# Seven block products in 18 of 44 weight units of a down projection (hybrid decoder block, one core)

## The chip, the cores and the metric

The kernel runs on 1 core of one Trainium2 chip. The metric is the device time of one execution in microseconds (us). Three executions of the kernel before took 1677.74, 1678.96 and 1675.05 us, median 1677.74 us. The profile comes from one further execution, which took 1675.62 us.

## The reference

One decoder layer, 256 tokens, model width 2048, feed-forward width 5632, all in float32: two token mixers, then a gated MLP with a short causal convolution, then a gate on a per-layer embedding. The change touches the MLP's last product, its residual sum, and the code that makes its left operand `h`:

```
h   = gelu(causal_conv3(x @ w_gate)) * (x @ w_up)     # 256 x 5632
ffn = h @ w_down                                      # 5632 x 2048
x   = layer_norm(ALPHA * x + ffn)
x   = x + sigmoid(x @ w_ple_gate) * (p @ w_ple_proj)
```

## The kernel before

All weights come from DRAM in 284 **units** of 128 x 2048 floats (1 MB) in one array `wu`, in the order in which they are used. TensorE (PE) works on a float32 value as a sum of a rounded part `hi` and a remainder `lo`, and forms three of the four products of two such sums. `prep` (L120) prepares a unit in two halves of 128 x 1024: SyncE (SP) loads `raw` (L126), ScalarE (ACT) copies it to `hi` (the copy is L104), VectorE (DVE) writes `lo = raw - hi` (L130). `unit` (L138) prepares up to unit u+2 before unit u is used. Four `raw` buffers hold two units, six `hi` and six `lo` buffers hold three. Nothing else is in front of PE: it waits only for `hi` and `lo`.

**The MLP** makes 44 blocks of 128 channels of `h`, number n = 0 to 43. For each, 16 K tiles of `w_gate` and of `w_up` go through PE into `psg` and `psu`, GpSimd (POOL) copies edge columns (`gp`, L998), DVE and ACT do convolution, gelu and product, and a tile `hT` gets the block's hi and lo parts for 256 tokens (L1013 is the last DVE operation).

**The down projection** is `residual("dn", ...)` (L831) with `x_half` (L251). It runs units 224 to 267, in two halves `nh` = 0 and 1 of the output's columns, 22 units each, i = 0 to 21. Unit i of a half holds the K tiles 2i and 2i+1 (256 channels of `h`) against 1024 output columns. `x_mm` (L223, the matmul is L237) does 24 matmuls for a unit: 2 K tiles, 2 halves of 128 tokens, 2 halves of 512 columns, and the three products ah*hi, ah*lo, al*hi; each has a 128 x 128 block of `h` as weights and 512 columns of the unit moving. Four PSUM banks collect the four blocks 128 tokens x 512 columns of a half. At its end `ev` (L834) does z = ALPHA*z + bank (L838) and the layer norm's statistics (L839) on DVE for each bank. `z` is the residual stream; its two tiles of 1 MB come back from the DRAM copy `x1d` with the layer norm's gains `lnb` (2 MB more) in `mid2` (L1020), which SP issues after unit i = 4 of the first half. The operands of the embedding's projection (`praw`, `pTr`; `ple_prep`, L859) are loaded at i = 17 of the second half. The last two units of that half are worked bank by bank (the tail), so that the layer norm's chain (L751 to L762), the transposes `ptl` (L765) and the embedding's products (`pp`) lie between the last matmuls. Then the gate's units follow (`pg`).

Each engine works its instructions in program order; a DMA that SP or POOL issues waits in that engine's order too. The order on SP is that of the program, the others' is a scheduler's.

Of the kernel before, what the change touches and what calls it, by code (L numbers as in the profile page):

```python
# [9 lines left out]
F32 = mybir.dt.float32  # L10
F32R = mybir.dt.float32r
# [3 lines left out]
ALU = mybir.AluOpType  # L15
# [4 lines left out]
P = 128  # L20
# [3 lines left out]
NF = DFF // P  # L24
# [4 lines left out]
ALPHA = 2 ** 0.25  # L29
# [12 lines left out]
LPAD = 24  # L42
XSTAT = (*range(32, 64), *range(120, 136), *range(224, 284))
S8W = 2048
WH = 1152
HSTEP = 48

# [5 lines left out]
def tile_block(ctx: ExitStack, tc: tile.TileContext, wu, wfv, wpp, xT_in, x_in, pT_in, wlr,  # L53
               chan, gnorm, lng, ident_in, mask_in, cmask_in, out):
    nc = tc.nc
# [4 lines left out]
    ring = ctx.enter_context(tc.tile_pool(name="ring", bufs=4))  # L60
# [33 lines left out]
    def t2(name):  # L94
        return sm.tile([P, 512], F32, tag="t2", bufs=6, name=name)

    def mmtile(name):
        return pmm.tile([P, 512], F32, tag="mm", name=name)

    def mxtile(name):  # L100
        return pmx.tile([P, 512], F32, tag="mx", name=name)

    def copy(o, i, scale=1.0):
        nc.scalar.activation(o, i, AF.Copy, bias=0.0, scale=scale)  # L104
# [12 lines left out]
    n_prep = [0]  # L117
    ready = {}

    def prep():  # L120
        u = n_prep[0]
        n_prep[0] += 1
        his, los = [], []
        for h in range(2):
            raw = ring.tile([P, 1024], F32, tag="raw", bufs=4, name=f"raw{u}_{h}")
            nc.sync.dma_start(raw, wu[u, :, h * 1024:(h + 1) * 1024])  # L126
            hi = w_tile("hi", F32R, f"hi{u}_{h}", u)
            copy(hi, raw)
            lo = w_tile("lo", F32R, f"lo{u}_{h}", u)
            nc.vector.tensor_tensor(lo, raw, hi.bitcast(F32), ALU.subtract)  # L130
            his.append(hi)
            los.append(lo)
        ready[u] = (his, los)
# [90 lines left out]
    def x_mm(banks, w, a, toks, first, last, cs=(0, 1), part=None):  # L224
# [3 lines left out]
        for t in toks:  # L228
            ah = a[:, t * P:t * P + P]
            al = a[:, 256 + t * P:256 + t * P + P]  # L230
            for i, (x, v) in enumerate(((ah, hi), (ah, lo), (al, hi))):
                for c in cs:
                    bs = banks[t][c]
                    m = 512 // len(bs)
                    for j in range(len(bs)) if part is None else (part,):
                        o = c * 512 + j * m
                        nc.tensor.matmul(bs[j][:, 0:m], lhsT=x, rhs=v[:, o:o + m],  # L237
                                         start=first and i == 0, stop=last and i == 2)

    mixers = []  # L240

    def pull(n):
# [6 lines left out]
                    mixers.pop(0)  # L249

    def x_half(name, act, K, evac, pulls=0, head=0, tail=0, mid=None, done=None, end=None,  # L251
               fine=False):
# [12 lines left out]

        us = [unit() for _ in range(head)]
        for t in range(2):
            for i, w in enumerate(us):
                mm(i, w, (t,))
        for i in range(head, n - tail):  # L270
            mm(i, unit(), (0, 1))
            pull(pulls)
            if mid is not None and i == mid[1]:
                mid[0]()
        us = [unit() for _ in range(tail)]

        def tail_mm(t, c, i):
            mm(n - tail + i, us[i], (t,), (c,))
            if i == tail - 1:
                evac(t, c, banks[t][c][0])  # L280

        if end is not None:
            end(tail_mm)
            return
        for t in range(2):
            for c in range(2):
                bs = banks[t][c]
                for j, ps in enumerate(bs):
                    for i, w in enumerate(us):
                        mm(n - tail + i, w, (t,), (c,), j)  # L290
                    if len(bs) == 1:
                        evac(t, c, ps)
                    else:
                        evac(t, c, ps[:, 0:256], (256 * j, 256 * j + 256))
            if done is not None:
                done(t)
# [531 lines left out]

        return stat, norm, turn

    def residual(name, act, K, zs, stats, mid, done=None, end=None):  # L831

        for nh in range(2):
            def ev(t, c, ps, nh=nh):  # L834
                g = 2 * nh + c
                zc = zs[t][:, g * 512:g * 512 + 512]
                with tc.high_priority(P_STAT):
                    nc.vector.scalar_tensor_tensor(zc, zc, ALPHA, ps, ALU.mult, ALU.add)  # L838
                    nc.vector.bn_stats(stats[t][:, g, :], zc)  # L839
            x_half(f"{name}{nh}", act, K, ev, tail=2 if nh == 1 else 0, mid=(mid[nh], 4 if nh == 0 else K // 2 - 5),  # L840
                   done=done if nh == 1 else None, end=end if nh == 1 else None)

    def affine(zs, gb_, after, gs=range(4)):
        for t in range(2):
# [130 lines left out]
    for i in range(2):  # L975
        nc.gpsimd.memset(gp[i][:, 0:2], 0.0)
    hT = [None] * 11

    def lt(shape, dt, name):
        return late.tile(shape, dt, name=name)  # L980
# [9 lines left out]
    for n in range(NF):  # L990
        if n % 4 == 0:
            hT[n // 4] = (s8 if n < 40 else lt)([P, 4, 512], F32R, name=f"hT{n // 4}")
        psg = gate_up(f"psg{n}")
        g = gp[n % 2]
        comb(psg, g[:, 2:258])
        cw = [chn[:, c_cw + j * NF + n:c_cw + j * NF + n + 1] for j in range(3)]
        for i in range(2):
            nc.gpsimd.tensor_copy(g[:, 258 + i:259 + i], g[:, 129 - i:130 - i])  # L998
# [12 lines left out]
        dst = hT[n // 4][:, n % 4, :]  # L1011
        copy(dst[:, 0:256], y)
        nc.vector.tensor_tensor(dst[:, 256:512], y, dst[:, 0:256].bitcast(F32), ALU.subtract)  # L1013
        if n >= 4:
            pull(1)

# [3 lines left out]
    def mid2():  # L1020
        for t in range(2):
            nc.sync.dma_start(z2[t], x1d[t])
        gain[1] = load_gain(1)

    x2T = [s8([P, 4, 512], F32R, name=f"x2T{g}") for g in range(4)]
# [4 lines left out]
            pb.extend(ple_proj(1, *pq[0]))  # L1030
        ln_out(z2, st2, t, x2T, c_g2, c_b2, "l2", P_LN2[t])

    residual("dn", hT, NF, z2, st2, (mid2, lambda: pq.append(ple_prep(1))), done2)
    pp = [s8([P, 2, 1024], name=f"ppk{i}") for i in range(2)]
    for t in range(2):
        for c in range(2):
# [112 lines left out]
```

## Time and profile before

| | |
|---|---|
| time of the profiled execution | 1675.62 us |
| span of the profile | 1673.6 us |
| median of three other executions | 1677.74 us |
| granted TensorE clock | 1.0 in all slices |
| PE, DVE, ACT, POOL busy | 99%, 66%, 50%, 2% |
| dn matmuls, first to last start | 1056, from 1331.4 to 1572.7 us |

About 2.0 us of the profiled time lie outside its span. "Busy" counts an engine's instructions; PE's matmuls overlap one another, so what a matmul costs is read from the distance of starts, not from its length. In the views an operation stands as line, engine, operation, output<-input with buffer numbers left out, and the shapes; "idle before <-" is the time in which an engine waited and what it waited for.

### The profile page before, as it was taken

The page shows a single profiled execution, that of the slowest core. Times are in us where ns is not written, and L with a number is a line of the kernel's source. Part 1 is how long each engine was busy: PE and PEld are TensorE (multiplying, and loading weights), DVE is VectorE, ACT ScalarE, POOL GpSimd, SP SyncE. Part 2 cuts the span into 40 slices and gives each one's busy share as a digit, 9 for nine tenths or more (in the row PEclk, how much of TensorE's full clock was granted, in tenths as well). Part 3 has the DMA queues.
Part 4 walks back from the last instruction along what each step waited for, and adds up shares of the span by engine and source line. Part 5 has one row for each costly group of instructions (what it writes and reads, how often), then busy time and mean ns, then how long its engine had stood idle before and what let it go on. Part 6 is the DMA issues. An engine that isn't in the chain of part 4 may idle for free.

```text
span 1673.6 us, 23839 instructions
## 1 busy us (share of the span) xinstructions
PE 1663.7 (99%) x9035; PEld 1442.6 (86%) x9035; DVE 1097.6 (66%) x1588; ACT 833.7 (50%) x1200; POOL 36.0 (2%) x123
## 2 busy tenths in 40 slices
PE   9999999999999999999999999999999999999998
PEld 8888888888888888888888888888888888888887
DVE  6576658768756657774687776677676644545774
ACT  5655545545555554443465545555545434334633
POOL 0100000000000000000010000000000000000000
PEclk9999999999999999999999999999999999999999
DMA  7765555555555556567746665555555575566454
GB/s 268 258 201 165 165 188 184 180 177 177 184 180 175 167 191 196 193 195 279 237 159 201 219 221 193 193 195 191 194 196 193 194 295 191 193 194 206 154 182 170
DMA packets 91426, 330.22 MB, mean 197 GB/s; under 512 B 10232, under 2 KB 11904, under 8 KB 89904
## 3 DMA queue, kind: packets, MB, share of 16 engines
q1 hardware_dynamic: 90528, 324.51, 58.3%
q0 software_dynamic: 784, 4.20, 0.7%
q8 instruction: 70, 1.15, 0.3%
q14 instruction: 44, 0.36, 0.1%
HBM read 323.42 MB, written 5.25 MB: 196 GB/s over the span
## 4 chain that ended last, share of the span: by engine, by line
PE 97%; DVE 1%; ACT 0%; DMA 0%; SPq 0%; issue 0%; POOL 0%; ACTq 0%
PE dn L237 14%; PE psu L193 9%; PE psg L193 9%; PE psm L193 7%; PE gr L237 5%; PE gv L237 5%; PE wo L237 5%; PE pg L237 5%; PE psu L195 5%; PE psg L195 5%; PE psm L195 3%; PE psa L193 3%; PE fv L344 2%; PE psfk L193 2%; PE psq L193 2%; PE psfq L193 2%
## 5 line engine op out<-in xcount | busy, mean ns | idle before, releaser
L130 DVE TENSOR_TENSOR lo<-raw,hi 128x1024 fp32r<-128x1024 f32 x568 | 694.0, 1224 | 484.6 <-ACT hi L104 483.5
L104 ACT ACTIVATE hi<-raw 128x1024 fp32r<-128x1024 f32 x568 | 601.8, 1060 | 706.9 <-issue 260.0
L193 PE MATMUL psu<-x1T,hi 128*128 128x512 f32 x688 | 236.0, 389 | 0.0
L193 PE MATMUL psg<-x1T,hi 128*128 128x512 f32 x672 | 230.5, 389 | 0.0
L237 PE MATMUL dn<-hi,hT 128*128 128x512 f32 x704 | 190.0, 389 | 0.0
L195 PE MATMUL psu<-x1T,lo 128*128 128x256 f32 x688 | 189.9, 276 | 0.0
L195 PE MATMUL psg<-x1T,lo 128*128 128x256 f32 x672 | 185.5, 276 | 0.0
L193 PE MATMUL psm<-xT,hi 128*128 128x512 f32 x512 | 175.8, 391 | 0.0
L237 PEld LDWEIGHTS dn<-hi,hT 128*128 128x128 f32 x704 | 132.1, 188 | 27.4
L193 PEld LDWEIGHTS psu<-x1T,hi 128*128 128x128 f32 x688 | 129.1, 188 | 26.8
L193 PEld LDWEIGHTS psg<-x1T,hi 128*128 128x128 f32 x672 | 126.2, 188 | 26.2
L195 PE MATMUL psm<-xT,lo 128*128 128x256 f32 x512 | 141.4, 276 | 0.0
L195 PEld LDWEIGHTS psu<-x1T,lo 128*128 128x128 f32 x688 | 129.1, 188 | 0.0
L195 PEld LDWEIGHTS psg<-x1T,lo 128*128 128x128 f32 x672 | 126.1, 188 | 0.0
L193 PEld LDWEIGHTS psm<-xT,hi 128*128 128x128 f32 x512 | 96.1, 188 | 19.8
L237 PE MATMUL dn<-lo,hT 128*128 128x512 f32 x352 | 109.7, 389 | 0.0
L195 PEld LDWEIGHTS psm<-xT,lo 128*128 128x128 f32 x512 | 96.1, 188 | 0.1
L193 PE MATMUL psa<-oT,hi 128*128 128x512 f32 x256 | 87.8, 389 | 0.0
L237 PEld LDWEIGHTS dn<-lo,hT 128*128 128x128 f32 x352 | 66.1, 188 | 13.7
L237 PE MATMUL gv<-hi,xT 128*128 128x512 f32 x256 | 72.3, 394 | 0.0
L237 PE MATMUL gr<-hi,xT 128*128 128x512 f32 x256 | 72.1, 394 | 0.0
L195 PE MATMUL psa<-oT,lo 128*128 128x256 f32 x256 | 70.7, 276 | 0.0
(247 smaller groups left out, 2423.3 us busy)
## 6 DMA issues: line engine op xcount, KB each, us to landing
raw<-in_wu_dram SPq DMA_DIRECT2D x568, 512.0 KB, 4.6
fvraw<-in_wfv_dram SPq DMA_DIRECT2D x14, 524.0 KB, 8.9
lnb<-in_lng_dram SPq DMA_DIRECT2D x4, 1024.0 KB, 12.0
z<-in_x_dram SPq DMA_DIRECT2D x2, 1024.0 KB, 7.6
praw<-in_wpp_dram SPq DMA_DIRECT2D x4, 512.0 KB, 3.8
x1d<-z POOLq DMA_DIRECT2D x2, 1024.0 KB, 7.5
z<-x1d SPq DMA_DIRECT2D x2, 1024.0 KB, 7.6
xraw<-in_xT_dram SPq DMA_DIRECT2D x7, 256.0 KB, 7.7
```

What stands on the lines that cost most here:

```text
L104: nc.scalar.activation(o, i, AF.Copy, bias=0.0, scale=scale)
L130: nc.vector.tensor_tensor(lo, raw, hi.bitcast(F32), ALU.subtract)
L193: nc.tensor.matmul(ps, lhsT=hi[i // 8 if hoff == 0 else 0][:, w0 % 1024:w0 % 1024 + P], rhs=a[:, kt % 4, :], start=first and i == 0, stop= ...
L195: nc.tensor.matmul(ps[:, 256:512], lhsT=lo[i // 8 if hoff == 0 else 0][:, w0 % 1024:w0 % 1024 + P], rhs=a[:, kt % 4, 0:256], start=False, ...
L237: nc.tensor.matmul(bs[j][:, 0:m], lhsT=x, rhs=v[:, o:o + m], start=first and i == 0, stop=last and i == 2)
L344: nc.tensor.matmul(fbk[t][c][:, 0:n], lhsT=x, rhs=w[:, o:o + n], start=kt == 0 and i == 0, stop=kt == 15 and i == 2)
```

## The change

In nine units of each half (i = 2, 4, ... 18; `DNP`) the 256 x 1024 block of `w_down` and the 256 x 256 block of `h` are taken as 2 x 2 matrices of blocks, and the product is formed from **seven** block products instead of eight (the Winograd form of Strassen's scheme). Each takes three matmuls of 128 x 128 by 128 x 512, so such a unit has 21 in place of 24. Three of the seven add into the half's own banks; four (`ms`) collect in banks of their own over the nine units, so that all eight banks of PSUM are in use from i = 2 to 18.

- `prep_seven` makes the operands. ACT copies 512 + 1024 columns to `hi` and, for the weights' four combinations, 2 x 1024 to a tile `ts`; DVE makes `lo` of 512 + 1024, four combinations of 512 in place in `raw`, and 2 x 1024 `lo` parts of `ts`. `ts` takes the wide S8 buffers.
- h's four combinations are made once, in the MLP, at n = 5, 9, ... 37: four DVE operations of 128 x 128, an ACT copy and a DVE subtraction of 128 x 512, and two POOL writes of 256 KB to DRAM (`hsd`). Each seven unit loads them back with two POOL DMAs of 256 KB, into the free upper halves of its first `hi` and `lo`.
- `joined` adds the four banks onto z after i = 18: one ACT copy and eight DVE operations of 128 x 512. z is scaled by ALPHA there, so `ev` only adds.
- `mid2` loads z alone; the gains' 2 MB move to i = 17 of the second half, behind `ple_prep`.

```
+DN0 = 224
+DNP = tuple(range(2, 20, 2))
...
+    def prep_seven(u):
...
+            n = 512 * (h + 1)
+            copy(hi[:, 0:n], raw[:, 0:n])
+            nc.vector.tensor_tensor(lo[:, 0:n], raw[:, 0:n], hi[:, 0:n].bitcast(F32),
+                                    ALU.subtract)
...
+        sums[u](his[0][:, 512:1024], los[0][:, 512:1024])
+        (b11, b12), (b21, b22) = [(r[:, 0:512], r[:, 512:1024]) for r in raws]
+        nc.vector.tensor_tensor(b11, b12, b11, ALU.subtract)
+        nc.vector.tensor_tensor(b12, b22, b12, ALU.subtract)
+        nc.vector.tensor_tensor(b22, b22, b11, ALU.subtract)
+        nc.vector.tensor_tensor(b21, b21, b22, ALU.subtract)
+        ts = []
+        for h, raw in enumerate(raws):
+            t = s8([P, 2, 1024], F32R, name=f"ts{u}_{h}")
+            copy(t[:, 0, :], raw)
+            nc.vector.tensor_tensor(t[:, 1, :], raw, t[:, 0, :].bitcast(F32), ALU.subtract)
+            ts.append(t)
...
+    def seven(banks, ms, w, act, kt, first, last):
...
+        for ps, (xh, xl), (vh, vl) in (
+                (ms[0], x[0], (h0[:, 0:512], l0[:, 0:512])),
+                (banks[0][0][0], x[1], (h1[:, 0:512], l1[:, 0:512])),
+                (banks[0][1][0], s[3], (h1[:, 512:1024], l1[:, 512:1024])),
+                (ms[1], s[0], t1_), (ms[2], s[2], t3), (ms[3], s[1], t2_),
+                (banks[1][0][0], x[2], t4)):
+            m = any(ps is p for p in ms)
+            for i, (a, v) in enumerate(((xh, vh), (xh, vl), (xl, vh))):
+                nc.tensor.matmul(ps, lhsT=a, rhs=v, start=m and first and i == 0,
+                                 stop=m and last and i == 2)
...
+            if i in ws:
...
+                seven(banks, ms, unit(), act, 2 * i, i == ws[0], i == ws[-1])
+                if i == ws[-1]:
+                    joined(ms)
+            else:
+                mm(i, unit(), (0, 1))
...
-                    nc.vector.scalar_tensor_tensor(zc, zc, ALPHA, ps, ALU.mult, ALU.add)
+                    if ws:
+                        nc.vector.tensor_tensor(zc, zc, ps, ALU.add)
...
+            def joined(ms, zp=zp):
+                p1, p5, p7, p6 = ms
+                u = t2("ju")
+                copy(u, p1)
...
+                onto(0, 0, p1)
+                plus(u, u, p6)
+                onto(0, 1, u)
+                plus(u, u, p7)
+                onto(1, 0, u)
+                plus(u, u, p5)
+                onto(1, 1, u)
+                plus(zp(0, 1), zp(0, 1), p5)
...
+            nc.gpsimd.dma_start(h.bitcast(F32), hsd[j, :, 0, :])
+            nc.gpsimd.dma_start(l.bitcast(F32), hsd[j, :, 1, :])
...
+        if n % 2 == 1 and n // 2 in DNP:
+            sf = t2("hs")
+            x_sums(before[0], y, sf)
...
+                nc.gpsimd.dma_start(hsd[DNP.index(n // 2), :, i, :], sp.bitcast(F32))
...
+    def mid2b():
+        pq.append(ple_prep(1))
         gain[1] = load_gain(1)
...
+    residual("dn", hT, NF, z2, st2, (mid2, mid2b), done2, ws=DNP)
```

Where the changed order matters:

**DVE, first half, one seven unit with the regular unit behind it.** Before, a unit is two rows of `lo`, four for two units:

```order
L130 TENSOR_TENSOR lo_0_14039<-raw_0_14035,hi_0_14037 128x1024
L130 TENSOR_TENSOR lo_1_14045<-raw_1_14041,hi_1_14043 128x1024
L130 TENSOR_TENSOR lo_0_14075<-raw_0_14071,hi_0_14073 128x1024
L130 TENSOR_TENSOR lo_1_14081<-raw_1_14077,hi_1_14079 128x1024
```

Now (L133, L140 to L143 and L148 are the seven unit's, the two L165 the next, regular unit's):

```order
L133 TENSOR_TENSOR lo_0_13436<-raw_0_13433,hi_0_13435 128x512
L140 TENSOR_TENSOR raw_0_13433<-raw_0_13433 128x512
L141 TENSOR_TENSOR raw_0_13433<-raw_1_13439,raw_0_13433 128x512
L133 TENSOR_TENSOR lo_1_13442<-raw_1_13439,hi_1_13441 128x1024
L148 TENSOR_TENSOR ts_0_13451<-raw_0_13433,ts_0_13451 128x1024
L142 TENSOR_TENSOR raw_1_13439<-raw_1_13439,raw_0_13433 128x512
L165 TENSOR_TENSOR lo_0_13482<-raw_0_13478,hi_0_13480 128x1024
L143 TENSOR_TENSOR raw_1_13439<-raw_1_13439 128x512
L165 TENSOR_TENSOR lo_1_13488<-raw_1_13484,hi_1_13486 128x1024
L148 TENSOR_TENSOR ts_1_13454<-raw_1_13439,ts_1_13454 128x1024
```

Ten rows stand where four stood. The seven unit's first `raw` buffer is free for the next seven unit's load only after L142, its last operand `ts_1` is made behind both halves of the regular unit.

**SP, around the loads of z.** Before:

```order
L126 DMA raw_1_12907<-in_wu_dram 128x1024
L1022 DMA z_12746<-x1d 128x2048
L1022 DMA z_12747<-x1d 128x2048
L856 DMA lnb_12939<-in_lng_dram 128x2048
L856 DMA lnb_12940<-in_lng_dram 128x2048
L126 DMA raw_0_12943<-in_wu_dram 128x1024
```

Now (L128 loads a seven unit's half, L161 a regular one's; the numbers are the units'):

```order
L128 DMA raw230_0_13026<-in_wu_dram 128x1024
L128 DMA raw230_1_13032<-in_wu_dram 128x1024
L1151 DMA z20_12846<-x1d_7192 128x2048
L1151 DMA z21_12847<-x1d_7192 128x2048
L161 DMA raw231_0_13073<-in_wu_dram 128x1024
L161 DMA raw231_1_13079<-in_wu_dram 128x1024
L128 DMA raw232_0_13109<-in_wu_dram 128x1024
```

The two `lnb` loads are gone from this place. Before, the two issues of z waited for the MLP's last matmul. Now the first waits for PE's last product with `ts` of unit 226 and the second for PE's product with the first `ts` of unit 228 (z takes buffers that `ts` tiles held), and `raw231` and what follows stand behind them on SP.

**DVE, at the end of the second half's seven units** (i = 18 is unit 264; `ju` is the sum that `joined` carries). Now:

```order
L926 SCALAR_TENSOR_TENSOR z_12846<-z_12846,dn1m_13842 128x512
L930 TENSOR_TENSOR ju<-ju,dn1m_13845 128x512
L926 SCALAR_TENSOR_TENSOR z_12846<-z_12846,ju 128x512
L930 TENSOR_TENSOR ju<-ju,dn1m_13844 128x512
L926 SCALAR_TENSOR_TENSOR z_12847<-z_12847,ju 128x512
L930 TENSOR_TENSOR ju<-ju,dn1m_13843 128x512
L930 TENSOR_TENSOR z_12846<-z_12846,dn1m_13843 128x512
L926 SCALAR_TENSOR_TENSOR z_12847<-z_12847,ju 128x512
```

These eight rows did not exist; they stand ahead of `lo` of units 266 and 267, the two units of the tail.

More of the change, by code (lines that the diff above doesn't have):

```diff
@@ L118, in tile_block @@
     ready = {}
+    sums = {}
+    def prep_seven(u):
+        raws, his, los = [], [], []
+        for h in range(2):
+            raw = ring.tile([P, 1024], F32, tag="raw", bufs=4, name=f"raw{u}_{h}")
+            nc.sync.dma_start(raw, wu[u, :, h * 1024:(h + 1) * 1024])
+            hi = w_tile("hi", F32R, f"hi{u}_{h}", u)
+            lo = w_tile("lo", F32R, f"lo{u}_{h}", u)
+            n = 512 * (h + 1)
+            copy(hi[:, 0:n], raw[:, 0:n])
+            nc.vector.tensor_tensor(lo[:, 0:n], raw[:, 0:n], hi[:, 0:n].bitcast(F32),
+                                    ALU.subtract)
+            raws.append(raw)
+            his.append(hi)
+            los.append(lo)
+        sums[u](his[0][:, 512:1024], los[0][:, 512:1024])
[10 more added lines that the diff above has]
+            ts.append(t)
+        ready[u] = (his, los, ts)
     def prep():
@@ L122, in prep @@
         n_prep[0] += 1
+        if u in sums:
+            prep_seven(u)
+            return
         his, los = [], []
@@ L238, in x_mm, with x_sums @@
                                          start=first and i == 0, stop=last and i == 2)
+    def seven(banks, ms, w, act, kt, first, last):
+        (h0, h1), (l0, l1), ts = w
+        a0, a1 = [act[k // 4][:, k % 4, :] for k in (kt, kt + 1)]
+        x = [(a[:, t * P:t * P + P], a[:, 256 + t * P:256 + t * P + P])
+             for a, t in ((a0, 0), (a1, 0), (a1, 1))]
+        s = [(h0[:, 512 + i * P:512 + i * P + P], l0[:, 512 + i * P:512 + i * P + P])
+             for i in range(4)]
+        t1_, t3, t4, t2_ = [(t[:, 0, o:o + 512], t[:, 1, o:o + 512])
+                            for t in ts for o in (0, 512)]
+        for ps, (xh, xl), (vh, vl) in (
[8 more added lines that the diff above has]
+                                 stop=m and last and i == 2)
+    def x_sums(ae, ao, o):
+        d = [o[:, i * P:i * P + P] for i in range(4)]
+        a11, a21, a12, a22 = ae[:, 0:P], ae[:, P:256], ao[:, 0:P], ao[:, P:256]
+        for dst, a, b, op in ((d[0], a21, a22, ALU.add), (d[1], d[0], a11, ALU.subtract),
+                              (d[2], a11, a21, ALU.subtract), (d[3], a12, d[1], ALU.subtract)):
+            nc.vector.tensor_tensor(dst, a, b, op)
     mixers = []
@@ L270, in x_half @@
         for i in range(head, n - tail):
-            mm(i, unit(), (0, 1))
+            if i in ws:
+                if i == ws[0]:
+                    ms.extend(mmtile(f"{name}m{j}") if j % 2 == 0 else mxtile(f"{name}m{j}")
+                              for j in range(4))
+                seven(banks, ms, unit(), act, 2 * i, i == ws[0], i == ws[-1])
[3 more added lines that the diff above has]
+                mm(i, unit(), (0, 1))
             pull(pulls)
@@ L977, in tile_block, with h_sums, load @@
     hT = [None] * 11
+    hsd = dr.tile([len(DNP), P, 2, 512], F32, name="hsd")
+    before = [None]
+    def h_sums(i):
+        j = DNP.index(i)
+        def load(h, l):
+            nc.gpsimd.dma_start(h.bitcast(F32), hsd[j, :, 0, :])
+            nc.gpsimd.dma_start(l.bitcast(F32), hsd[j, :, 1, :])
+        return load
+    for nh in range(2):
+        for i in DNP:
+            sums[DN0 + nh * (NF // 2) + i] = h_sums(i)
     def lt(shape, dt, name):
@@ L1013, in tile_block @@
         nc.vector.tensor_tensor(dst[:, 256:512], y, dst[:, 0:256].bitcast(F32), ALU.subtract)
+        if n % 2 == 1 and n // 2 in DNP:
+            sf = t2("hs")
+            x_sums(before[0], y, sf)
+            for i, nm in enumerate(("hsh", "hsl")):
+                sp = sm.tile([P, 512], F32R, tag="t2", bufs=6, name=nm)
+                if i == 0:
+                    sh = sp
+                    copy(sp, sf)
+                else:
+                    nc.vector.tensor_tensor(sp, sf, sh.bitcast(F32), ALU.subtract)
+                nc.gpsimd.dma_start(hsd[DNP.index(n // 2), :, i, :], sp.bitcast(F32))
+        before[0] = y
         if n >= 4:
```

24 lines of the change are left out of this document (17 added, 7 removed).

## The prediction

> **What bounds the kernel now.** First the page: how busy each engine is, and the chain that ended last.
>
> ```profile
> PE 1663.7 (99%) x9035; PEld 1442.6 (86%) x9035; DVE 1097.6 (66%) x1588; ACT 833.7 (50%) x1200; POOL 36.0 (2%) x123
> PE 97%; DVE 1%; ACT 0%; DMA 0%; SPq 0%; issue 0%; POOL 0%; ACTq 0%
> ```
>
> PE is the end of the chain for 97% of the span: a matmul less is time less, as long as PE's operands still come in time. So the second view is who waits for whom from 1325 to 1600 us, the down projection and what follows (waiter <- awaited: us in all, times, longest).
>
> ```profile
> DVE lo L130 <- ACT hi L104: 122.5, 85, 6.1
> ACT hi L104 <- PE dn L237: 120.9, 75, 1.7
> ACT hi L104 <- DMA raw<-in_wu_dram: 14.4, 8, 6.3
> PE ptl L765 <- DVE z L759: 0.6, 1, 0.6
> ```
>
> DVE waits for ACT, ACT for a `hi` buffer that PE still reads; PE itself waits 0.6 us once. Preparation stands up against the three units' buffers. The busy times by stretch say how much room it has (columns: length; PE, PEld, DVE, ACT, POOL busy; clock; DMA share; GB/s):
>
> ```profile
> 1340.00:1360.00 20.00, 20.00 (x90) 16.53 (x89) 7.35 (x6) 6.21 (x6) 0.00 (x0) 1.00 0.87 330
> 1380.00:1400.00 20.00, 20.00 (x90) 16.57 (x89) 8.78 (x8) 7.79 (x8) 0.00 (x0) 1.00 0.58 191
> ```
>
> In the steady state DVE works 8.8 of 20 us. The change spends that room.
>
> **What it removes.** 18 units lose 3 matmuls each, 54 in all, of the same shape. Their price is read from ACT, which starts one copy for every 12 matmuls:
>
> ```profile
> 1342.57 1.06 ACT L104 ACTIVATE hi<-raw 128x1024 fp32r<-128x1024 f32 x1 [1.66 <-PE dn L237]
> 1345.29 1.06 ACT L104 ACTIVATE hi<-raw 128x1024 fp32r<-128x1024 f32 x1 [1.66 <-PE dn L237]
> ```
>
> 2.72 us for 12 is 0.2267 us for one, so 54 x 0.2267 = **12.2 us** go. [...]
>
> **What it adds in the steady state.** A seven unit and the regular one behind it are 45 matmuls, 45 x 0.2267 = 10.2 us. The durations:
>
> ```profile
> L130 DVE TENSOR_TENSOR lo<-raw,hi 128x1024 fp32r<-128x1024 f32 x85 | 104.0, 1225 | 117.6 <-ACT hi L104 117.6
> L104 ACT ACTIVATE hi<-raw 128x1024 fp32r<-128x1024 f32 x85 | 90.2, 1061 | 136.4 <-PE dn L237 120.9 <-DMA raw<-in_wu_dram 12.6 <-issue 2.9
> L848 DVE TENSOR_TENSOR z<-z,lnb 128x512 f32<-128x512 f32 x24 | 16.0, 685 | 0.2
> L104 ACT ACTIVATE x2T<-lny 128x512 fp32r<-128x512 f32 x8 | 4.9, 633 | 0.0
> 1590.91 3.56 DVE L130 TENSOR_TENSOR lo<-raw,hi 128x1024 fp32r<-128x1024 f32 x3
> 1594.39 2.01 DVE L848 TENSOR_TENSOR z<-z,lnb 128x512 f32<-128x512 f32 x3
> ```
>
> The last two rows show that back to back three of 1024 columns start 3.48 us from the next operation, 1.16 each, and those of 512 somewhat under 0.67. By the order DVE has five operations of each size per pair: 5 x (0.65 to 0.685) + 5 x (1.16 to 1.225) = 9.1 to 9.6 us. ACT has one copy of 512 and five of 1024: 0.63 + 5.3 = 5.9 us. So DVE would be busy 89 to 94% of PE's 10.2 us. It fits, but only if DVE hardly waits; that is where the forecast hangs.
>
> What makes it wait is a loop through `raw`: the next seven unit's first half is loaded into the buffer that L142 frees. From issue it takes the landing L, ACT's copy of 512 (0.63), four DVE operations of 512 and two of 1024 up to the next L142: L + 0.63 + 2.6 to 2.75 + 2.3 to 2.45, L + 5.7 with a middle value, 5.8 with the hand-overs. Landings of 512 KB of weights, over the whole kernel, in the steady stretch 1380 to 1440 and in the crowded one 1328 to 1372 (the last two rows: minimum, median, maximum):
>
> ```profile
> raw<-in_wu_dram SPq DMA_DIRECT2D x568, 512.0 KB, 4.6
> DMA to landing us min/median/max: 3.5/3.7/5.0
> DMA to landing us min/median/max: 3.6/5.2/12.9
> ```
>
> L = 3.7 gives a loop of 9.5, L = 4.6 one of 10.4; it equals PE's 10.2 at L = 4.4. Loads per pair are 2.1 MB of weights and 0.5 MB of h's sums, 257 GB/s where 191 are moved now and 330 were moved over 1340 to 1360, so I take L near 4.2, nearer to the steady row than to the crowded one, and keep 3.5 to 6 for the range.
>
> There is also a lead to use up. Where PE sets the pace, `hi` of the regular unit's second half is free 18 matmuls into the seven unit two units back (6.1 us ahead of the seven unit's start); a copy, a `lo` and the `lo` of `ts_1` later (3.4 us) the last operand is ready, and it is first needed after 15 matmuls (3.4 us): 6.1 us early, some 5.5 with hand-overs. The second half has eight periods, so it stalls 8 x (loop - 10.2) - 5.5. In the first half the loads of z take most of the lead:
>
> ```profile
> z<-x1d SPq DMA_DIRECT2D x2, 1024.0 KB, 7.6
> lnb<-in_lng_dram SPq DMA_DIRECT2D x4, 1024.0 KB, 12.0
> 1360.71 1.06 ACT L104 ACTIVATE hi<-raw 128x1024 fp32r<-128x1024 f32 x1 [6.25 <-DMA raw<-in_wu_dram]
> ```
>
> Before, the 4 MB of z and gains made ACT wait 6.25 us once, and PE not at all. Now z's second issue waits for PE's 15th matmul of unit 228, 13.6 us after the start of 226, with `raw231` behind it on SP; a landing like z's later, at some 20 us, preparation goes on, and the last operand of unit 232 is ready at about 33.3, needed at 3 x 10.2 + 3.4 = 34.0. That is 0.7 us early, then five periods: the stall is 5 x (loop - 10.2) - 0.7. At L = 4.2 both are nothing; since an error of half a us in that walk falls through to PE, I put **0.7** for the first half and **0.4** for the second with the turn between them.
>
> **What it adds elsewhere.** `joined` is eight DVE operations of 512, 5.3 us, ahead of `lo266`. By the same walk `lo266_0` is ready 10.9 us after unit 264 begins and needed at 11.8: cover 0.9, so **0.3** expected; bounds nothing and 5, since the gains' 2 MB, at 330 GB/s 6.4 us, now also stand on SP ahead of `raw266`. At the layer norm the 0.6 us wait of before stays in kind: z's norm now stands on DVE behind the last `ev`, 12 products of the embedding cover it, but the second transposes wait for a chain of some seven DVE and ACT steps of 0.4 us with 9 products (2.0 us) as cover; worked through, 1.0 to 1.5 us of waits, **0.5** more, bounds -0.6 and 2.
>
> ```profile
> L774 DVE TENSOR_SCALAR lny<-ptl,chn 128x128 f32<-128x128 f32 x16 | 6.3, 401 | 0.8 <-ACT lny L772 0.6 <-PE ptl L765 0.2
> ```
>
> In the MLP nine blocks get four DVE operations of 128 x 128, one of 512 and a copy:
>
> ```profile
> L597 DVE TENSOR_TENSOR kq<-gq,e 128x128 f32<-128x128 f32 x56 | 13.6, 283 | 0.0
> 1200.00:1328.00 128.00, 128.00 (x754) 113.56 (x754) 89.30 (x128) 65.04 (x95) 4.09 (x22) 1.00 0.58 194
> ```
>
> 4 x 0.283 + 0.685 = 1.8 us in every fourth block (21.8 us there, with 6.6 idle): **0**; without that cover it would be 9 x 1.8 = 16 us. h's loads come on POOL's own queue; the nearest row is a POOL write of the same size, and below it POOL's only frequent instruction:
>
> ```profile
> ppd<-ppo POOLq DMA_DIRECT2D x4, 256.0 KB, 2.7
> L998 POOL COPY gp<-gp x88: 183/220/1196, 869.9 to 1329.0; 128x1 f32<-128x1 f32 x88
> ```
>
> 2.7 us against a lead of 14 (the `hi` and `lo` buffers are free 12.9 us before the unit begins, the seventh matmul, 1.4 us into it, is the first user): **0**.
>
> **Sum.** -12.2 + 0.7 + 0.4 + 0.3 + 0.5 = -10.3 us: 1675.6 becomes 1665.3 for an execution like the profiled one (span 1673.6, 2.0 outside it). That one is 2.1 us under the median 1677.7, which becomes **1667.4**. All times below are on the median's scale.
>
> **Rivals.**
> 1. All is covered: 1665.5. For it: PE never waited for operands here, even under 4 MB. Against it: four new tight places, each within 1 us.
> 2. The landings govern in part. L = 5.0 gives 10.8, a stall of 5 x 0.6 - 0.7 = 2.3 and none in the second half; L = 5.2 gives 3.3 + 0.9. Or the gains' 2 MB delay `raw266` by 2 to 5 us. 1669.5 to 1674. For it: the crowded stretch's median. Against it: 257 GB/s are well under 330.
> 3. The same loop, longer, eats the gain: 13 periods x excess - 6.2 equals 10.9 (12.2 less 1.3) at an excess of 1.3 us, L = 5.7. From there the kernel is no faster, from L = 6.0 slower: at L = 6.5, excess 2.1, the stalls are 21 us and the time 1687. What speaks for it: once DVE and `raw` are late, four halves are requested within about 5 us, 2.1 MB, and 1 MB loads took 7.6 and 12. Against it: the first half requested is the first served, and a slow loop asks for less.
> 4. POOL's issues starve. POOL's copies `gp` take 183 ns at least and 1196 at most, which is one DVE operation of 1024 more. If an issue needed a pause of DVE, one in 10 us, and each pause let one pass, a unit's second load would land 9.6 + 10.2 + 2.7 = 22.5 us after its buffer is free, 8 late, once in each half (PE's own wait then gives DVE pauses): 16 us, 1683. [...]
> 5. The change doesn't remove what it says: excluded, since PE's order holds 1002 dn matmuls, 54 fewer.
>
> **Chances.** Forecast (1666 to 1669.5) 0.43; rival 1 0.13; rival 2 0.18; no change within 0.2% (1674.4 to 1681.1: L of 5.5 to 6.0) 0.09; slower, rival 3 0.14 and rival 4 0.03, together 0.17. A measurement of this kernel tells about 0.2%, 3.4 us, from no change. So faster 0.74, same 0.09, slower 0.17. The range 1664.3 to 1681 leaves out the slower cases and a gain beyond all 54 matmuls.
>
> **What would show it.** Right: dn's matmuls span some 229 to 231 us in place of 241.3, PE's waits in it sum to under 2 us, DVE is 88 to 95% busy between units 228 and 242, and `raw` lands in 3.7 to 4.6 us. Wrong: PE waiting for `ts` or its `lo` at every second unit (rival 3; at the last units of a half only, rival 2), for `hi266`, `lo266` (tail), or for h's loads (rival 4); matmuls of seven units at another distance than 0.227 us; `psu` or `psg` waiting for DVE in the MLP.

## The result and the profile after

The changed kernel took 1686.32 us (median of 4, 1684.89 to 1686.97) beside 1678.26 us of the kernel before on the same chip: 1.0051 times as long, 95% interval 1.0033 to 1.0068, **slower by some 8 us** where 10.3 us less had been forecast. The profiled execution took 1686.97 us, span 1685.2.

The page's rows for busy time and for the chain that ended last:

```profile
PE 1660.2 (99%) x8981; PEld 1435.2 (85%) x8981; DVE 1197.6 (71%) x1757; ACT 867.2 (51%) x1247; POOL 65.0 (4%) x177
PE 85%; DMA 7%; DVE 5%; ACT 2%; issue 1%; SPq 0%; POOL 0%; ACTq 0%; DVEq 0%
raw<-in_wu_dram SPq DMA_DIRECT2D x568, 512.0 KB, 4.6
hi<-hsd POOLq DMA_DIRECT2D x18, 256.0 KB, 4.0
hsd<-hsh POOLq DMA_DIRECT2D x9, 256.0 KB, 5.7
```

The 54 matmuls are gone (8981 for 9035). But PE holds 85% of the chain where it held 97%: DMA, DVE and ACT have come into it. "Busy" hides this, since the modelled length of a matmul, 389 ns, reaches over a short pause. The waits from 1325 to 1600 us show who is late now:

```profile
ACT hi L106 <- DMA raw<-in_wu_dram: 83.6, 50, 4.7
ACT ts L106 <- DVE raw L143: 26.1, 16, 2.8
DVE lo L133 <- ACT hi L106: 22.2, 29, 2.9
DVE raw L141 <- DMA raw<-in_wu_dram: 9.6, 11, 1.8
PEld dn1m L293 <- DVE ts L148: 6.5, 7, 1.4
```

Before, ACT waited 14.4 us for loads and 120.9 us for PE. Now it waits 83.6 us for loads, and PE waits for `ts`. Preparation used to wait for PE; now PE waits for preparation.

The chain of waits, from 1385 to 1425 us in order of time (start, length, what), shows the cause as a loop. (A unit is loaded as two `raw` halves; in what follows "the first load" and "the second load" of a unit are these, and "landing" is the time from a load's issue to its data being in place. The two halves of the down projection are the 22 units each of `nh` = 0 and 1.) One turn of it, with the steps just ahead:

```profile
1398.43 0.68 DVE raw L142
1399.12 1.15 DVE lo L165
1400.27 0.02 issue
1400.28 5.67 DMA raw<-in_wu_dram
1405.95 0.02 issue
1405.97 0.04 ACTq L106
1406.01 0.04 issue
1406.05 1.07 ACT hi L106
1407.13 0.02 issue
1407.15 1.23 DVE lo L133
1408.38 0.07 DVE ts L148
1408.44 0.98 issue
1409.43 0.68 DVE raw L142
1410.11 1.15 DVE lo L165
1411.26 0.02 issue
1411.27 5.71 DMA raw<-in_wu_dram
```

From one load to the next, 1400.28 to 1411.27, are 11.0 us: a seven unit's second load 5.67, its copy 1.07, its `lo` 1.23, `lo` of `ts_0` (here 0.07 and the 0.98 called issue), the combination L142 0.68, and `lo` from the regular unit's first load 1.15, whose `raw` buffer takes the next load. PE needs 10.2 us for the pair. There is nothing of PE in the loop: with four `raw` buffers it turns by itself. SP's issues of one turn, ACT's first copy, and the stretch in the windows view:

```profile
1399.18 1.43 SPq L128 DMA_DIRECT2D raw<-in_wu_dram  x2
1402.02 1.60 SPq L161 DMA_DIRECT2D raw<-in_wu_dram  x2
```

```profile
1403.17 0.63 ACT L106 ACTIVATE hi<-raw 128x512 fp32r<-128x512 f32 x1 [1.17 <-DMA raw<-in_wu_dram]
```

```profile
1400.00:1420.00 20.00, 18.10 (x78) 14.09 (x77) 16.25 (x19) 10.47 (x13) 2.13 (x4) 1.00 0.71 236
```

The four loads of a pair are asked for within 4.5 us. The one asked for first lands 4.0 us later, the second, which closes the loop, 5.7.

From unit 234 to 242 SP asks for a seven unit's first load every 11.0 us. In the second half (units 250 to 264) it is every 11.0 to 12.0 us, 11.5 at the mean. There the loop closes twice through the first load, not the second; the head of one such turn, without the short issue steps (the next first load is asked for at 1498.79):

```profile
1486.65 0.69 DVE raw L142
1487.39 5.47 DMA raw<-in_wu_dram
1492.97 0.64 ACT hi L106
```

In these two turns the first load lands in 5.47 and 6.08 us, not in 4.0.

What PE does with it is seen in the starts of the first matmul of each seven unit. From unit 226 they are 10.20 us apart four times, then 12.1, 12.2, 11.1 and 11.0; in the second half 11.5, 10.2, 10.2, 10.6, 11.3, 10.9, 12.1 and 11.2. So 45 matmuls that don't wait take 10.2 us, as forecast (0.2267 us each), and in the profiled execution the time went as follows. "Covered" is a version shown below, in which PE waits for nothing; the cells are the distance between starts, rounded, and the last two rows go up to the span's end. The last row also holds units 224 and 225, 10.9 us in both.

| stretch, us | after | covered | lost |
|---|---|---|---|
| unit 226 to 242 (eight pairs) | 87.1 | 81.6 | 5.5 |
| unit 242 to 248 (the turn between the halves) | 35.1 | 32.0 | 3.1 |
| unit 248 to 264 (eight pairs) | 88.0 | 81.6 | 6.4 |
| unit 264 to the first gate matmul (tail and layer norm) | 34.9 | 28.2 | 6.7 |
| gate matmuls to the end | 95.2 | 94.6 | 0.6 |
| first dn matmul to the end | 351.1 | 328.9 | 22.2 |

The kernel before took 342.2 us for the last row. So 13.3 us were there to be gained, 22.2 are lost, and 8.9 remain as loss; the medians differ by 8.1. The spans of the profiled executions differ by 11.6, because the changed one began dn 2.7 us later, at 1334.1. That is no part of the change: the MLP's first `psg` matmul already starts 2.7 us later (851.5 for 848.8), ahead of the first DMA of h's combinations (925.8). First dn starts in the profiles of this study lie between 1331.1 and 1335.9, and the kernel before itself took 1675.4 to 1675.6 us when its mean granted clock was 1.0 and 1675.9 to 1681.9 when it was 0.997 to 0.999. The profile of before happened to be one at 1.0.

The worst place is the tail. PE's rows there, then the clock by stretches of 2 us (length; PE, PEld, DVE, ACT, POOL busy; clock; DMA share; GB/s):

```profile
1565.68 0.41 PE L272 MATMUL pp<-pw,pTs 128*128 128x512 f32 x1
1567.64 0.50 PE L272 MATMUL pp<-pw,pTs 128*128 128x512 f32 x1 [1.54 <-DVE ju L930]
1569.92 1.24 PE L272 MATMUL dn<-hi,hT 128*128 128x512 f32 x4 [1.78 <-ACT hi L106]
```

```profile
1566.00:1568.00 2.00, 0.46 (x2) 0.19 (x1) 1.90 (x4) 0.00 (x0) 0.00 (x0) 1.00 1.00 410
1568.00:1570.00 2.00, 0.22 (x2) 0.09 (x1) 1.97 (x4) 1.06 (x1) 0.00 (x0) 1.00 1.02 418
1570.00:1572.00 2.00, 2.00 (x6) 1.28 (x7) 2.00 (x3) 1.75 (x2) 0.00 (x0) 0.74 0.72 293
1572.00:1574.00 2.00, 2.00 (x6) 1.61 (x5) 1.99 (x3) 1.43 (x2) 0.00 (x0) 0.50 0.71 199
1574.00:1576.00 2.00, 2.00 (x9) 1.61 (x9) 0.87 (x1) 0.57 (x1) 0.00 (x0) 0.91 0.81 244
```

PE waits for `joined` to free a bank, then for `hi266`, and is busy for 0.7 us of 4. Then the granted clock falls to 0.5, for some 3 us in all, which by these rows costs an estimated 0.52 + 1.0 + 0.18 = 1.7 us more. In experiments 1, 6 and 8, where PE has no wait in the tail, the clock is 1.00 from 1560 to 1590 us.

### The profile page after: what moved, and what is told of

It is laid out like the page before. It is cut to its first block, busy times and chain, and to the rows that moved or that the text cites. A ratio compares the mean times of both kernels' runs of the same rounds, so it can differ in the third digit from the quotient of the medians.

```text
span 1685.2 us, 24107 instructions
## 1 busy us (share of the span) xinstructions
PE 1660.2 (99%) x8981; PEld 1435.2 (85%) x8981; DVE 1197.6 (71%) x1757; ACT 867.2 (51%) x1247; POOL 65.0 (4%) x177
## 3 DMA queue, kind: packets, MB, share of 16 engines
q8 instruction: 70, 1.15, 0.3%
## 4 chain that ended last, share of the span: by engine, by line
PE 85%; DMA 7%; DVE 5%; ACT 2%; issue 1%; SPq 0%; POOL 0%; ACTq 0%; DVEq 0%
PE psu L228 9%; PE psg L228 9%; PE psm L228 7%; DMA raw<-in_wu_dram 6%; PE gr L272 5%; PE gv L272 5%; PE wo L272 5%; PE pg L272 5%; PE psu L230 5%; PE psg L230 5%; PE psm L230 3%; PE psa L228 3%; PE fv L417 2%; PE psfq L228 2%; PE psfk L228 2%; PE psq L228 2%
## 5 line engine op out<-in xcount | busy, mean ns | idle before, releaser
L106 ACT ACTIVATE hi<-raw 128x1024 fp32r<-128x1024 f32 (+1 forms) x568 | 592.6, 1046 | 656.1 <-issue 219.4
L165 DVE TENSOR_TENSOR lo<-raw,hi 128x1024 fp32r<-128x1024 f32 x532 | 649.4, 1223 | 357.8 <-ACT hi L106 356.5
L272 PE MATMUL dn<-hi,hT 128*128 128x512 f32 x416 | 117.8, 393 | 2.7 <-ACT hi L106 1.8
L272 PEld LDWEIGHTS dn<-hi,hT 128*128 128x128 f32 x416 | 78.6, 189 | 20.0 <-ACT hi L106 2.1
L272 PE MATMUL wo<-hi,mT 128*128 128x512 f32 x256 | 70.2, 390 | 0.0
L272 PE MATMUL pg<-hi,x2T 128*128 128x512 f32 (+1 forms) x256 | 69.0, 379 | 0.0
## 6 DMA issues: line engine op xcount, KB each, us to landing
lnb<-in_lng_dram SPq DMA_DIRECT2D x4, 1024.0 KB, 10.9
```

The source lines that it names most:

```text
L272: nc.tensor.matmul(bs[j][:, 0:m], lhsT=x, rhs=v[:, o:o + m], start=first and i == 0, stop=last and i == 2)
```

## The experiments

**Theory.** With four `raw` buffers the pair of units goes round a loop through one load that is longer than PE's 10.2 us. **Rivals.** DVE is full, its work and hand-overs make 11.0 us whatever the buffers; or the loads take the time from one another, h's among them.

### 1. A fifth raw buffer

```
-            raw = ring.tile([P, 1024], F32, tag="raw", bufs=4, name=f"raw{u}_{h}")
+            raw = ring.tile([P, 1024], F32, tag="raw", bufs=5, name=f"raw{u}_{h}")
...
-WH = 1152
+WH = 1088
```

Also five buffers in place of six for the tiles t1 and t2.

> The changed kernel with a fifth raw buffer; the room comes from the small tiles (five t1 and five t2 buffers in place of six) and from hi buffers of 1088 columns in place of 1152. Theory (raw loop): the 11.0 us period of a seven unit with its regular neighbour is a loop through the second half's raw buffer: lo of the regular unit's first half 1.14, landing of the seven unit's second half 5.7, the combination that reads it and the wait for its hi 1.1, lo 1.14, lo of ts_0 1.14, third combination 0.68, in all 11.0. With one more buffer the load is issued about half a unit earlier, the period falls to PE's 10.2, the stalls of 5.5 and 6.4 us in the two halves fall under 1.5 each, and the time falls by 8 to 12 us against the changed kernel, to about 1675 to 1678. Rival (DVE is full: 9.5 us of work and hand-overs that can't be filled): period stays 10.9 to 11.0, time about 1686. Rival (the loads compete for bandwidth): landings lengthen with the earlier issue, period stays near 11.0.

1670.49 us (median of 4) beside 1678.06, ratio 0.995 (0.993 to 0.9969): 15.8 us under the changed kernel, more than the theory's upper end. The eight pairs of the second half take 81.6 us, exactly 10.2 each; turn and tail have no wait left either. The first half keeps 4.1 us, from unit 234 to 240. The second half, by the windows view and the landing row of `raw` (minimum, median, maximum) from 1464 to 1546:

```profile
1470.00:1540.00 70.00, 70.00 (x310) 57.98 (x309) 65.58 (x73) 41.91 (x44) 7.54 (x14) 1.00 0.79 264
DMA to landing us min/median/max: 3.6/5.9/10.9
```

DVE works 65.58 of 70 us, 94%, and PE doesn't wait: DVE isn't full. The loads land no sooner than in the changed kernel (5.9 at the median, 5.5 there) while more bytes are moved (264 GB/s): bandwidth isn't the bound either. One load more in flight is what was missing. Both rivals fall here.

### 2. No loads of h's combinations

```
-        sums[u](his[0][:, 512:1024], los[0][:, 512:1024])
...
-        s = [(h0[:, 512 + i * P:512 + i * P + P], l0[:, 512 + i * P:512 + i * P + P])
-             for i in range(4)]
+        s = [x[0], x[1], x[2], x[0]]
```

> The changed kernel without POOL's loads of h's combinations in the down projection (the four products take blocks of h itself in their place; the sums are still made in the MLP). Raw loop: h's loads are issued some 3 us ahead of the first raw load and have mostly landed, so the second half's landing falls by 0.4 us at most and the period stays at 10.6 or more, time 1682 to 1686. Rival (bandwidth or POOL's issue): landing back to 3.7, period 10.2, time under 1676.

One execution, 1687.45 us. The eight pairs take 86.8 and 85.7 us (87.1 and 88.0 with the loads). `raw` from 1385 to 1435:

```profile
DMA to landing us min/median/max: 3.8/5.6/6.8
```

5.6 us at the median without h's 9.4 MB. The stretch as a whole:

```profile
1385.00:1435.00 50.00, 46.60 (x199) 36.67 (x198) 40.85 (x45) 26.32 (x28) 0.00 (x0) 1.00 0.55 177
```

That is 177 GB/s, less than the 191 of the kernel before, whose loads land in 3.7 us. So neither h's bytes nor the mean rate makes the landing long. What differs is the spacing: here four loads within 4.5 us, there one every 2.72. SP asks for a seven unit's first load every 11.1 to 11.5 us here, no sooner than with h's loads. The rival (h's bytes, or POOL's issue) fails; 2.3 us in the second half may be theirs, one execution doesn't tell. The time came out above the theory's 1682 to 1686; 1.8 us of it lie ahead of the first dn matmul, which starts at 1335.9.

### 3. No lo part of the second ts tile

```
-            nc.vector.tensor_tensor(t[:, 1, :], raw, t[:, 0, :].bitcast(F32), ALU.subtract)
+            if h == 0:
+                nc.vector.tensor_tensor(t[:, 1, :], raw, t[:, 0, :].bitcast(F32), ALU.subtract)
...
-        t1_, t3, t4, t2_ = [(t[:, 0, o:o + 512], t[:, 1, o:o + 512])
-                            for t in ts for o in (0, 512)]
+        t1_, t3, t4, t2_ = [(t[:, 0, o:o + 512], t[:, 1 - j, o:o + 512])
+                            for j, t in enumerate(ts) for o in (0, 512)]
```

> The changed kernel without DVE's lo part of the second ts tile (the matmuls that read it take the hi part again): 18 operations of 1.22 us less, from a place outside the raw loop. Raw loop: the operation stands in DVE's pause while raw lands, so the period stays 10.8 to 11.0; PE's waits for it at the end of a seven unit become waits for ACT's copy, time 1683 to 1686. Rival (DVE full): DVE's work falls to 8.3 us, period 10.2, time about 1673 to 1676.

One execution, 1682.66 us. The pairs take 84.4 and 83.4 us: their stall falls from 11.8 to 4.7 us, where the theory said unchanged and the rival none. Both were wrong: a place outside the loop was not without effect. But the turn and the tail grew, to 37.7 and 37.5 us (35.1 and 34.9 in the changed kernel), so that from the first dn matmul to the end only 2.2 us are gained; why they grew isn't shown. The last operand of a seven unit is ready one operation earlier, and its `raw` buffer is free earlier too, so this edit cuts DVE's work and loosens the loop at once; by itself it doesn't tell the two apart.

### 4. The gains behind raw of the tail

```
     def mid2b():
         pq.append(ple_prep(1))
+
+    def mid2c():
         gain[1] = load_gain(1)
...
+            if name == "dn1" and i == n - 3:
+                mid2c()
```

> The changed kernel with the layer norm's gains (2 MB) loaded after i = 19 of the second half, behind raw of units 266 and 267, in place of i = 17, ahead of them. Theory (the tail's two waits, 1.5 and 1.8 us, and the clock of 0.66 behind them come from the gains ahead of raw266): hi266's wait goes, the clock stays 1.0, 3 to 5 us less, about 1682. Rival (joined holds DVE and so the tail): the wait for ju stays 1.5 us and hi266's wait too, change under 1 us.

1685.9 us (median of 4), ratio to before 1.0045 (1.0029 to 1.0061), against 1.0051 of the changed kernel: no change that can be told. PE's waits in the tail became four for `lo` and one for `hi` (1.18 us), and the clock still fell to 0.5. From unit 264 to the gate are 37.9 us, no less than the 34.9 of the changed kernel. So moving the gains' 2 MB doesn't free the tail. The chain now goes through the second `praw` load (5.22 us to landing), its copy and its `lo`, and the tail's last `raw` load, asked for only behind them at 1560.60 (6.56 us). The two `praw` loads take two of the four `raw` buffers just there. With five buffers the tail has no wait, the gains still in front.

### 5. The control: five buffers in the kernel before

The edit of experiment 1 on the kernel before.

> The kernel before with the fifth raw buffer and the same smaller tiles: the control for the first run. Raw loop: PE waited nowhere for a load there, so the time stays within 2 us of the kernel before's 1678. Rival (a fifth buffer helps all the kernel's phases): some 8 us faster, 1670.

1677.67 us beside 1677.59, ratio 1.0 (0.9991 to 1.001; 10 and 13 executions). The fifth buffer and the smaller tiles do nothing where PE doesn't wait; all of experiment 1's gain is in the down projection.

### 6. Five buffers, and z loaded by POOL

```
-            nc.sync.dma_start(z2[t], x1d[t])
+            nc.gpsimd.dma_start(z2[t], x1d[t])
```

> The changed kernel with five raw buffers as in the first run, and the two loads of z issued by POOL in place of SP. What is left of PE's waits with five buffers (4.1 us around units 234 to 240) comes from raw231 and the loads behind it waiting on SP behind z: with z on POOL's queue the stall of the first half falls under 1 us and the time by 3 to 4, to about 1667. Rival (z's 2 MB take the bandwidth, whoever issues them): stall stays 3 to 4.5 us, time 1670.

**1663.4 us** (median of 4) beside 1677.59, ratio 0.9916 (0.9901 to 0.9931): 14.2 us faster than before, the best version of the study. All sixteen pairs take 10.20 us, and PE has no wait from the first dn matmul to the gate. In it ACT waits for PE again, and less for loads:

```profile
ACT hi L106 <- PE dn L272: 49.1, 37, 2.6
ACT hi L106 <- DMA raw<-in_wu_dram: 17.3, 15, 5.0
```

DVE's share from 1470 to 1540, and the landing of `raw` from 1380 to 1540:

```profile
1470.00:1540.00 70.00, 70.00 (x310) 57.96 (x309) 63.64 (x71) 41.28 (x44) 6.45 (x12) 1.00 0.81 271
DMA to landing us min/median/max: 3.6/6.0/10.8
```

So what was left of the first half's stall with five buffers was SP's order, z's issues with their wait for PE ahead of `raw231`, and not z's bytes, which are the same. Of the 7.1 us between the medians of experiments 1 and 6, 4.3 are seen in the profiles from the first dn matmul on, about what was expected. The profiles also differ by 4.5 us ahead of it (1335.5 and 1331.1); the mean clock of the two profiled executions was 0.997 and 1.0, and 0.91 in the first 20 us of experiment 1. That the rest of the 7.1 comes from there is argued, not shown.

### 7. z by POOL with four buffers

> The changed kernel with four raw buffers and z's loads issued by POOL. Raw loop with a lead: the first half begins with the full lead of about 5.5 us and stalls 8 x 0.8 less 5.5, 1 to 2 us in place of 6.7; the second half, which begins after joined and four evacuations (10.3 us of DVE), stalls 6 to 7 as before; time about 1681. Rival: no lead is left anyway, the first half stalls 5 us or more, time 1685 or more.

One execution, 1685.43 us; the pairs take 87.2 and 87.0 us. The rival's number was right, but not its reason. The chain shows unit 231's second load, asked for at 1355.44 beside z's, landing only after 12.83 us; PE waits 2.1 us in unit 230, and later stalls come anyway. That load was 7.1 us longer than the 5.7 of the loop, so by these rows an estimated 5 us of it were covered: there was a lead, and z's bytes took it. The first half's stall is as long with z on POOL (5.6 us) as on SP (5.5).

### 8. Seven products in every third unit

```
-DNP = tuple(range(2, 20, 2))
+DNP = tuple(range(2, 20, 3))
```

> The changed kernel with seven products in every third unit (i = 2, 5, ... 17; six of 22) in place of every second. 36 matmuls less than before, 8.2 us. Raw loop: three units are 15.6 us of PE, the loop with one more regular unit some 13.5, so the steady stretches have no stall; what is left are the turn and the tail, 3 to 6 us with the clock there; time 1673 to 1676. Rival (loops do not matter, joined and the tail cost all): 1678 or more.

1668.04 us (median of 4) beside 1677.59, ratio 0.9945 (0.9929 to 0.9962), with four buffers and nothing else changed. From one seven unit to the next are 15.64 us all ten times, PE waits nowhere, tail included, and the gain is 9.6 us where 36 matmuls are 8.2. With two regular units in between the same buffers and the same queue are enough. Both expectations were too slow: the tail needs no cure where the stretch ahead of it isn't late.

### 9. The second half first

```
-        for h in range(2):
+        for h in (1, 0):
             raw = ring.tile([P, 1024], F32, tag="raw", bufs=4, name=f"raw{u}_{h}")
...
+        raws, his, los = raws[::-1], his[::-1], los[::-1]
```

> The changed kernel with four raw buffers; a seven unit loads, copies and subtracts its second half before its first. Raw loop: the chain of 11.0 us (landing 5.7, hi copy 1.1, lo 1.2, lo of ts_0 1.05, third combination 0.7, lo of the regular unit 1.15) is replaced by one through the first half, requested last, whose copy is of 512 columns and whose lo is off the chain: landing 5.4 to 5.7, two combinations 1.4, the third or a lo 1.2, lo of ts_0 1.2, hand-overs: period 10.2 to 10.7, 3 to 8 us less stall in all, 1678 to 1683. Rival (the sum of DVE's work and hand-overs sets the period, in whatever order): 10.9 to 11.1 as before, 1685 or more.

One execution, 1693.29 us; the periods went up, to 11.6 and 11.4 us at the mean of the two halves, where the changed kernel has 10.9 and 11.0. Both expectations failed. The chain of waits shows another loop:

```profile
1403.23 5.45 DMA raw<-in_wu_dram
1408.68 0.02 issue
1408.70 0.04 ACTq L106
1408.74 0.04 issue
1408.78 1.07 ACT hi L106
1409.85 0.03 issue
1409.88 0.99 DVE lo L166
```

In three of the four turns from 1385 to 1440 us the loop now closes through a load of the regular unit (its `lo` is L166), and these land in 5.45 to 7.28 us. DVE's order changed with the edit, and so did the turn of the buffers; which of the two made the loads later isn't shown. It is no cure, but it counts against the rival of a full DVE: the same DVE work in another order gave another period.

### 10. Seven products in two of three units

```
-DNP = tuple(range(2, 20, 2))
+DNP = tuple(i for i in range(2, 19) if i % 3 != 1)
```

On the version of experiment 6.

> The version with five raw buffers and z on POOL's queue, with seven products in two of three units (i = 2, 3, 5, 6, ... 17, 18; 12 of 22) in place of every second. 72 matmuls less than the kernel before, 16.3 us. Theory (DVE is the next bound): three units are 66 matmuls, 15.0 us of PE, and 2 x 6.9 + 2.35 = 16.1 us of DVE, so DVE sets a period of 16.1 to 17: 7 to 14 us of stalls over twelve periods, and the time is not under 1663, 1664 to 1675. Rival (DVE's 94% were not near a bound): period 15.0, time about 1659.

One execution, 1696.89 us. The five periods of three units from i = 2 to 17 take 88.4 us in the first half and 90.5 in the second, 17.7 and 18.1 each, where the estimate for DVE was 16.1 to 17, and PE waits another 2.57 us at the layer norm. DVE was busy 43.6 of the 50 us from 1380 to 1430, less than in experiment 6. The granted clock was 0.90 in that stretch, with matmuls 0.41 to 0.43 us apart from 1424.8 to 1428.2 in place of 0.2267, so a part of the length is the clock's. So more seven units don't pay, but that DVE alone is the bound there is not shown; with five buffers `raw` is in that chain too (19% of it from 1395 to 1430).

## Why the prediction was wrong

**The step that failed first is the raw loop with its landing time.** The prediction had the mechanism, as its second and third rivals, and the break-even, "it equals PE's 10.2 at L = 4.4". It took L near 4.2, "nearer to the steady row than to the crowded one", and so a loop of 10.0; the loop was 11.0 us in the first half and 11.5 in the second. Two things were off. The prediction's loop goes through the first load. In the first half the chain goes through the second, which SP can issue only after one more `lo`: landing + 5.3 us, so that 4.9 would have been short enough; it landed in 5.7. And L was too short: the median of all from 1380 to 1440 was 5.5, and in the second half, where the loop twice was the predicted one, the first load took 5.47 and 6.08. The steady row, 3.7, was that of a kernel that asks for one load every 2.72 us; the change asks for four in a bunch. The reason against, "257 GB/s are well under 330", is about the mean and says nothing on four loads asked for within 4.5 us: at 177 GB/s, without h's loads, the median was still 5.6 (experiment 2).

**The lead is the second step that failed, and weighs as much.** With a loop of 11.0 the prediction's own sums give stalls of 3.3 and 0.9 us, and a kernel still some 7 us faster. Measured were 15.0 with the turn (5.5 + 3.1 + 6.4), where 1.1 had been put. In the second half a lead of 5.5 us was to pay for eight long periods. It was worked out for a stretch in which PE sets the pace, but that half starts behind `joined` and four evacuations with their statistics, 5.5 us of DVE each by the lengths of the operations: PE waits 0.8 us for an evacuation and 1.0 for `ts` in the first pair. What lead was left then was used up by unit 256: from a seven unit's first load to its first matmul are 14.5 us at unit 250 and 10.8 from 256 on. With 11.5 us the prediction's sum for this half is 8 x 1.3 - 5.5 = 4.9; measured were 9.5 with the turn. In the first half z takes the lead, as the prediction had it, but the stall is 5.5 where its sum at 11.0 has 3.3. How these remainders divide among the waits isn't shown.

**The tail** was put at 0.3 and the layer norm at 0.5. Against the version without waits they lost 6.7 us, of which the clock is an estimated 1.7. In the prediction's terms, against the kernel before less three matmuls (29.9 us), they cost 5.0, within the bounds but far from the 0.8 expected. The tail's walk gave a cover of 0.9 us for a preparation that is not late; here it came late into the tail. With five buffers, where it is on time, the tail has no wait. The clock had no term. Neither had the stretch from the gate to the end, which is 1.2 us longer than before; 0.7 of that is there in the version without waits too.

**What held:**
- 0.2267 us for a matmul: the unstalled pair takes 10.20 us. The 12.2 us are there, and experiment 6 collects them with 1 more: its first dn matmul to the end takes 13.3 us less than before. From unit 264 to the gate it is 1.7 us better than three matmuls less; from the gate on it is 0.7 worse. That the 1.7 come from the layer norm, where the 0.6 us wait is gone and the transposes no longer stand between the tail's matmuls, is argued, not shown.
- DVE at 89 to 94% of PE's time: 91 to 94% where it keeps pace, and enough (experiments 1 and 6). In the changed kernel itself, where 88 to 95% had been named as the sign of being right, it was 80% from 1380 to 1440, since preparation waited for loads.
- Nothing in the MLP: from the first `psg` to the first dn matmul are 482.6 us, before and after. (The prediction's "every fourth block (21.8 us there, with 6.6 idle)" is the time of two blocks; four have about twice the cover.)
- Nothing for h's loads: 4.0 us to landing at the median, no wait of PE for them. The fourth rival didn't come. From 1380 to 1440, with DVE 80% busy, the loads landed in 3.0 to 4.1 us.
- z on SP as a trouble of its own: 4.1 us with five buffers, gone when POOL issues it. With four buffers POOL's issuing doesn't help (experiment 7).

The chance for slower was 0.17, and the range ended at 1681. A loop without PE in it, whose break-even was 0.2 us from the value taken, deserved more.

## What to carry to other kernels

When an edit makes a unit's buffer live longer, write down the loop from one load into a buffer to the next, through every engine's order, and compare it with the time of the bottleneck engine; if that engine isn't in the loop, busy shares under 100% say nothing (here DVE was busy 80% where PE waited and 94% where it didn't). Take the landing time in such a loop for the bunch in which the new order will ask, not for the spacing of the old one (here 5.7 us in place of 3.7). Where the loop is longer, one buffer more or one regular unit more between is worth more than less work: here the same change went from 8 us slower to 14 us faster with a fifth buffer and two DMAs on another queue.

## What was not expected of the hardware

- Behind a stall of about 4 us at the tail the granted clock was 0.74, 0.50 and 0.91 in three stretches of 2 us: here a wait of PE cost nearly half as much again behind it, by the estimate above. It is seen again in experiment 4 (0.5 from 1570 to 1574).
- The clock in the first 100 us, where the changed and the unchanged kernel do the same work, differs from one execution to the next: 0.97 at the mean in the changed kernel's profile and 1.00 in that of before. Two slices of the changed kernel's start (length; PE, PEld, DVE, ACT, POOL busy; clock; DMA share; GB/s), then one of the kernel before's:

```profile
10.00:15.00 5.00, 2.90 (x16) 2.41 (x15) 3.08 (x3) 3.88 (x5) 0.00 (x0) 0.95 1.02 393
15.00:20.00 5.00, 5.00 (x25) 5.00 (x25) 4.29 (x6) 3.62 (x5) 0.00 (x0) 0.71 1.03 415
```

```profile
15.00:20.00 5.00, 5.00 (x34) 5.00 (x32) 4.80 (x6) 3.96 (x4) 0.00 (x0) 1.00 1.04 418
```

  The first dn matmul starts up to 4.9 us apart between profiles; so profiles of two kernels are compared from a common point behind the start.
